# Two MLPs that apply their norm after the first product, with split inputs made during the projection ahead, in a two-layer transformer kernel

## The chip, the cores and the metric

The kernel runs on one core of one Trainium2 chip, as one program. The metric is its device time in microseconds (us). All inputs and outputs are float32.

## The reference

The model has a first block of two layers (a mixer of neighbourhood attention and mLSTM heads, then an RWKV-7 mixer, each followed by an MLP) and a second block with a mixture of experts. What the change touches is the MLP of both layers and the end of the mixer ahead of it:

```python
def rms_norm(x, eps=NORM_EPS):
    xf = x.astype(jnp.float32)
    return (xf * lax.rsqrt(jnp.mean(xf * xf, axis=-1, keepdims=True) + eps)).astype(x.dtype)

def modulate(x, shift, scale):
    return rms_norm(x) * (1.0 + scale) + shift

def adaln(cond, w, b):
    return jnp.split(jax.nn.silu(cond) @ w + b, 6, axis=-1)

def squared_relu_mlp(h, w1, w2):
    return jnp.square(jax.nn.relu(h @ w1)) @ w2

# in each layer; the context only in the first
x = x + gt_a * o_l                # o_l ends with the mixer's output projection
x = x + gt_m * squared_relu_mlp(modulate(x, sh_m, sc_m), mlp_w1[layer], mlp_w2[layer])
ctx = ctx + cgt_a * o_c
ctx = ctx + cgt_m * squared_relu_mlp(modulate(ctx, csh_m, csc_m), mlp_w1[layer], mlp_w2[layer])
```

The width is 1024, the MLP's hidden width 4096. There are 512 tokens and 256 context tokens, with a shift, scale and gate of their own for the context.

## The kernel before

Activations lie transposed: 8 tiles `x[k]` of 128 features by 768 columns (512 tokens, then 256 of the context). `PARTS` is ((0, 512), (512, 768)), and layer 1's MLP works on the first part alone.

**Dense products.** Every float32 factor is split in a high and a low part, and a product is three matmuls: wh·ah, wh·al, wl·ah (`dense`, L493 in the trace). A weight tile (128 outputs, 1024 inputs) comes by DMA on SP's queue, ScalarE (ACT) makes `wh` (L471) and GpSimd (POOL) `wl` (L472). There are two buffers for split weights, so ACT can split the next tile only when TensorE (PE) has finished with the one before the last. Output tiles go to PSUM, into two accumulators of 768 columns (`wide`); in layer 0 a matmul for 512 and one for 256 columns follow each other on the same weight.

**Output projections.** `po` (layer 0, in `ab_mixer`) and `ro` (layer 1, in `rw_mixer`): eight output tiles each. Behind each, VectorE (DVE) adds gate times the tile to x (`residual`, L584), and `squares_add` squares x on ACT and sums over the eight tiles in `acc`. Behind the last, PE adds the sums over the partitions (`ssc`, L549), a chain of small steps on DVE and ACT takes the root (`rsv`, `rsy`), and PE turns it into rows (`rstd`, L559).

**MLP.** `modulate` makes eight pairs `ah`, `al` from x, the norm, scale and shift. Then four groups: eight up tiles of 128 hidden features, ReLU out of PSUM (ACT), squaring (DVE L616), split in `hh` (ACT) and `hl` (DVE L472), and eight down tiles `dn` with a residual each. The first two up tiles advance together (`dense_pair`).

**Conditioning passes.** Beside the MLP, `ada_side` makes the six adaLN vectors of the next layer. A step loads a tile of 128 x 1024 (`wside`, two buffers) and does one pass on DVE (L460, 128 x 1024 with a sum), or two for the vectors that the context needs too, 64 passes in 48 steps for each MLP. One step stands behind each up and down tile in the code.

**What sets the order.** The code is written stage by stage, and a scheduler (`tc`, tile pools) reorders instructions on each engine by when it reckons that their inputs and buffers are ready; each engine then takes its own list in order. A pool's memory comes free when the pool is closed. In `ab_mixer` the order of the heads is written by hand (`AB_ORDER`), and the splits `ch`, `cl` of the mixer's output `cat` come from the heads' own pool.

Of the kernel before, what the change touches and what calls it, by code (L numbers as in the profile page):

```python
# [10 lines left out]
F32 = mybir.dt.float32  # L11
# [4 lines left out]
ALU = mybir.AluOpType  # L16
# [275 lines left out]
PARTS = ((0, T), (T, TT))  # L292
NTD = 2
# [12 lines left out]
class Kern:  # L306
# [86 lines left out]
    def wide(self, name="a"):  # L393
        return self.acc.tile([128, TT], F32, tag="acc", name=self.uid(name))
# [47 lines left out]
    def ada_side(self, layer, pool):  # L442
# [8 lines left out]
        def step(j, f):  # L451
            n = 2 if j < 2 else 1
            if f == 0:
                self.ada[layer, j] = self.const.tile([128, 8, 2], F32, name=f"ada{layer}_{j}")
            out = self.ada[layer, j]
            w = pool.tile([128, D], F32, tag="wside", name=self.uid("wside"), bufs=2)
            nc.sync.dma_start(w, self.i[f"ada{layer}"][8 * j + f])
            for q in range(n):
                o = pool.tile([128, D], F32, tag="side", name=self.uid("side"), bufs=1)
                nc.vector.scalar_tensor_tensor(o, w, 1.0, cb[:, q, :], op0=ALU.mult, op1=ALU.mult, accum_out=out[:, f, q:q + 1])  # L460
            if f == 7:
# [4 lines left out]
        return [lambda j=j, f=f: step(j, f) for j in (1, 0, 2, 4, 3, 5) for f in range(8)]  # L466


    def split(self, src, hi, lo, eng=None):
        nc = self.nc  # L470
        nc.scalar.activation(hi, src, AF.Copy)  # L471
        (eng or nc.vector).tensor_tensor(lo, src, hi.bitcast(F32), op=ALU.subtract)  # L472
# [11 lines left out]
    def dense(self, ps, w, act, parts, k0=0, first=True, last=True):  # L484
# [96 lines left out]

    def residual(self, x, ps, gt, f, parts):
        for q, (a, b) in enumerate(parts):
            self.nc.vector.scalar_tensor_tensor(x[:, a:b], ps[:, a:b], gt[:, f, q:q + 1], x[:, a:b],  # L584
                                                op0=ALU.mult, op1=ALU.add)


    def mlp(self, layer, parts):
# [3 lines left out]
        with tc.tile_pool(name=f"mlp{layer}", bufs=2, reuse_waits="tile") as pool:  # L592
# [6 lines left out]
            act = self.modulate(self.x, sh, sc, parts, pool)  # L599
            w1, w2 = self.i[f"mlp1_{layer}"], self.i[f"mlp2_{layer}"]  # L600

            first = self.dense_pair("up", [w1[0], w1[1]], act, parts)

            def up(g):
                hid = []
                for f in range(8 * g, 8 * g + 8):
                    if first:
                        ps = first.pop(0)
                    else:
                        ps = self.wide("up")  # L610
                        self.dense(ps, self.load_w(w1[f], 1024), act, parts)
# [14 lines left out]
            for g in range(4):  # L626
# [3 lines left out]
                for f in range(KD):  # L630
# [9 lines left out]
            self.tb = 6  # L640


    def ab_mixer(self):
# [24 lines left out]
        with ExitStack() as st:  # L668
            cp = st.enter_context(tc.tile_pool(name="ab_c", bufs=1, reuse_waits="tile"))
            pool = self.abp = st.enter_context(tc.tile_pool(name="ab", bufs=2, reuse_waits="tile"))  # L670
# [263 lines left out]
            for f in range(8):  # L934
                self.tap("cat", cat[f], f)
            act2 = []
            for f in range(8):
                h = pool.tile([128, TT], F32R, tag="ah", name=self.uid("ch"), bufs=KD)
                l = pool.tile([128, TT], F32R, tag="al", name=self.uid("cl"), bufs=KD)
# [4 lines left out]
            acc = tmp("acc")  # L944
# [1512 lines left out]
```

## Time and profile before

| | |
|---|---|
| times of three runs, us | 3525.28, 3518.22, 3511.94 |
| median, us | 3518.22 |
| the profiled execution's own time, us | 3523.28 |
| its span, us | 3521.4 |
| mean granted clock of TensorE | 0.961 of full speed |
| PE busy | 3171.4 us (90%) |
| DVE busy | 1820.7 us (52%) |
| ACT busy | 1320.0 us (37%) |
| POOL busy | 913.9 us (26%) |
| DMA in 40 equal slices of the span | 34th and 35th 274 GB/s, 36th to 39th 420 or 421, last 312, most others 60 to 190 |

The span is the time between the first and the last instruction of the profiled execution; 1.9 us lie around it. An engine's busy time is a mean over stages with different limits: here PE, which is busy 90% of the span, is the engine that others wait for in most of them. Times in rows count from the start of the span.

### The profile page before, as it was taken

The numbers are of one execution on the slowest core, as the hardware profiler recorded it, in microseconds if no ns is written. First come the engines' busy times: TensorE is split into PE (matmuls) and PEld (weight loads), VectorE is DVE, ScalarE is ACT, GpSimd is POOL, SyncE is SP. The second block draws the span as 40 slices with busy tenths as digits, with TensorE's granted clock in tenths as the row PEclk, the third lists the DMA queues.
The fourth block names the chain that finished last, engine by engine and source line by source line (L and its number), as shares of the span: only waits on it lengthen the run. The fifth ranks groups of instructions, "written<-read, shape, count | busy, mean of one in ns | idle before, by whom it ended". The sixth has DMA issues, their size and how long they took to land. (4 is left out here: it accounts for less than half of the span.)

```text
span 3521.4 us, 56690 instructions
## 1 busy us (share of the span) xinstructions
PE 3171.4 (90%) x23582; PEld 2413.3 (69%) x23582; DVE 1820.7 (52%) x3073; ACT 1320.0 (37%) x2503; POOL 913.9 (26%) x467
## 2 busy tenths in 40 slices
PE   7989998899999789589999998799999899799887
PEld 4666887788888677377887876677778677333333
DVE  5476664862322975477777763864342654222213
ACT  3232453211222543377777774322233453100001
POOL 1111113222324423422223212344443324100000
PEclk9999999999999899699999998999999999899999
DMA  5222222552222233200000103473332228799997
GB/s 220 96 72 84 84 73 96 186 185 66 64 63 98 85 106 109 69 18 28 28 28 28 31 8 114 161 251 126 94 115 67 75 78 274 274 420 421 420 421 312
DMA packets 126321, 488.44 MB, mean 139 GB/s; under 512 B 13360, under 2 KB 23024, under 8 KB 101744
## 3 DMA queue, kind: packets, MB, share of 16 engines
q1 hardware_dynamic: 119936, 477.40, 37.9%
q8 instruction: 186, 3.05, 0.4%
q0 software_dynamic: 1184, 4.20, 0.3%
q10 hardware_dynamic: 4944, 3.21, 0.3%
q14 instruction: 71, 0.58, 0.1%
HBM read 455.92 MB, written 28.84 MB: 138 GB/s over the span
## 5 line engine op out<-in xcount | busy, mean ns | idle before, releaser
L472 POOL TENSOR_TENSOR wl<-w,wh 128x1024 fp32r<-128x1024 f32 (+1 forms) x259 | 626.4, 2420 | 1602.2 <-ACT wh L471 1458.0
L471 ACT ACTIVATE wh<-w 128x1024 fp32r<-128x1024 f32 (+1 forms) x259 | 266.8, 1032 | 909.5 <-PE dn L493 333.6
L493 PE MATMUL dn<-hh,wh 128*128 128x512 f32 (+1 forms) x768 | 235.5, 361 | 18.3 <-ACT hh L471 16.5
L493 PE MATMUL up<-ah,wl 128*128 128x512 f32 (+1 forms) x768 | 235.9, 361 | 6.3 <-POOL wl L472 6.2
L493 PE MATMUL up<-ah,wh 128*128 128x512 f32 (+1 forms) x768 | 235.2, 361 | 5.9 <-ACT ah L576 2.8
L493 PE MATMUL dn<-hl,wh 128*128 128x512 f32 (+1 forms) x768 | 235.1, 360 | 2.3 <-DVE hl L472 2.3
L493 PE MATMUL dn<-hh,wl 128*128 128x512 f32 (+1 forms) x768 | 234.5, 359 | 2.3 <-POOL wl L472 2.2
L493 PE MATMUL up<-al,wh 128*128 128x512 f32 (+1 forms) x768 | 234.8, 360 | 0.9 <-DVE al L577 0.9
L460 DVE SCALAR_TENSOR_TENSOR side<-wside,condb 128x1024 f32<-128x1024 f32 x128 | 194.7, 1521 | 69.7 <-DMA wside<-ada 68.5
L616 DVE TENSOR_TENSOR u<-u 128x768 f32<-128x768 f32 (+1 forms) x64 | 126.9, 1986 | 128.8 <-ACT u L615 128.8
L584 DVE SCALAR_TENSOR_TENSOR x<-dn,ada,x 128x512 f32<-128x512 f32 x96 | 60.5, 657 | 255.6 <-PE dn L493 255.6
L493 PEld LDWEIGHTS dn<-hh,wh 128*128 128x128 f32 x768 | 128.5, 191 | 42.4 <-ACT hh L471 18.1
L493 PEld LDWEIGHTS up<-ah,wl 128*128 128x128 f32 x768 | 128.8, 191 | 31.6 <-POOL wl L472 10.0
L493 PEld LDWEIGHTS up<-ah,wh 128*128 128x128 f32 x768 | 129.2, 192 | 29.8 <-ACT ah L576 3.9
L493 PEld LDWEIGHTS dn<-hl,wh 128*128 128x128 f32 x768 | 128.6, 191 | 26.3 <-DVE hl L472 4.2
L493 PEld LDWEIGHTS dn<-hh,wl 128*128 128x128 f32 x768 | 128.5, 191 | 25.1 <-POOL wl L472 3.1
L493 PEld LDWEIGHTS up<-al,wh 128*128 128x128 f32 x768 | 128.8, 191 | 24.2 <-DVE al L577 2.0
L471 ACT ACTIVATE hh<-u 128x768 fp32r<-128x768 f32 (+1 forms) x64 | 47.3, 740 | 220.9 <-DVE u L616 220.9
L493 PE MATMUL p<-ah,wh 128*128 128x512 f32 (+1 forms) x320 | 116.9, 394 | 2.2 <-ACT ah L576 1.2
L493 PE MATMUL rp<-xl,wh 128*128 128x512 f32 x368 | 109.2, 361 | 10.5 <-DVE xl L472 10.4
L493 PE MATMUL rp<-xh,wh 128*128 128x512 f32 x368 | 109.6, 364 | 9.1 <-ACT xh L471 7.9
L493 PE MATMUL p<-ah,wl 128*128 128x512 f32 x320 | 112.7, 381 | 2.1 <-POOL wl L472 2.1
(623 smaller groups left out, 7427.9 us busy)
## 6 DMA issues: line engine op xcount, KB each, us to landing
w<-mlp SPq DMA_DIRECT2D x128, 512.0 KB, 3.7
wside<-ada SPq DMA_DIRECT2D x96, 512.0 KB, 4.1
ew<-e_gate SPq DMA_DIRECT2D x45, 1024.0 KB, 19.8
ew<-e_up SPq DMA_DIRECT2D x41, 1024.0 KB, 21.1
ew<-e_down SPq DMA_DIRECT2D x39, 1024.0 KB, 19.8
wada<-ada SPq DMA_DIRECT2D x48, 512.0 KB, 3.6
ewm<-e_up SPq DMA_DIRECT2D x18, 1024.0 KB, 20.0
ewm<-e_down SPq DMA_DIRECT2D x18, 1024.0 KB, 19.8
```

The costliest lines, as they stand in the source:

```text
L460: nc.vector.scalar_tensor_tensor(o, w, 1.0, cb[:, q, :], op0=ALU.mult, op1=ALU.mult, accum_out=out[:, f, q:q + 1])
L471: nc.scalar.activation(hi, src, AF.Copy)
L472: (eng or nc.vector).tensor_tensor(lo, src, hi.bitcast(F32), op=ALU.subtract)
L493: nc.tensor.matmul(ps[:, a:b], ww[:, 128 * k:128 * k + 128], aa[:, a:b], start=(first and k == 0 and q == 0), stop=(last and k == nk - 1 a ...
L584: self.nc.vector.scalar_tensor_tensor(x[:, a:b], ps[:, a:b], gt[:, f, q:q + 1], x[:, a:b], op0=ALU.mult, op1=ALU.add)
L616: nc.vector.tensor_tensor(u[:, lo:hi], u[:, lo:hi], u[:, lo:hi], op=ALU.mult)
```

## The change

Three things change.

**The norm's place.** The pairs `ah`, `al` are no longer made by `modulate` but by `scaled`, one pair behind each residual of the output projection, from x times scale, without the norm and the shift. The shift is two more columns of the same pairs, so each up product carries 2 columns more; its product with the weights is read from PSUM behind the last column. The norm's matmuls stand among the first up products (`between`): the sums behind the sixth of eight steps (of 128 inputs) of the first up tile, the turning into rows behind the fourth of the second. DVE multiplies each up tile by the norm's rows `rn`, and ACT's ReLU adds the shift's product as its bias. In layer 1 the up products no longer have 512 columns in one matmul but 256 and 258 in two (`SHIFTED`), 768 more matmuls in all; in layer 0 they have 512 and 258. The first two up tiles of an MLP are put down one behind the other.

**Conditioning passes.** A step is now one pass, so 64 steps. One stands behind each up tile, two behind each down tile of the first two groups and one behind the others, each held behind the split or residual ahead of it (`issue_after`).

**The heads' pool.** In `ab_mixer` the heads' pool is closed after the last head, and the splits `ch`, `cl` come from a new pool `abo` behind it.

```diff
+SHIFTED = {1: ((0, T // 2), (T // 2, T + 2, T)), 2: ((0, T), (T, TT + 2))}
@@ ada_side @@
-        return [lambda j=j, f=f: step(j, f) for j in (1, 0, 2, 4, 3, 5) for f in range(8)]
+        parts = {j: 2 if j < 2 else 1 for j in range(6)}
+        return [partial(step, j, f, q, parts[j]) for j in (1, 0, 2, 4, 3, 5) for f in range(8) for q in range(parts[j])]
@@ dense @@
-                for a, b in parts:
-                    nc.tensor.matmul(ps[:, a:b], ww[:, 128 * k:128 * k + 128], aa[:, a:b],
+                for a, b, *at in parts:
+                    at = at[0] if at else a
+                    nc.tensor.matmul(ps[:, at:at + b - a], ww[:, 128 * k:128 * k + 128], aa[:, a:b],
@@ new @@
+    def scaled(self, layer, k, parts):
+        nc = self.nc
+        sh, sc = self.ada[layer, 3], self.ada[layer, 4]
+        n, x = parts[-1][1], self.x[k]
+        h, l = (self.actp.tile([128, n + 2], F32R, tag=tag, name=self.uid(tag)) for tag in ("ah", "al"))
+        c = sh[:, k, :] if len(parts) == 2 else sh[:, k, 0:1].to_broadcast([128, 2])
+        nc.scalar.activation(h[:, n:], c, AF.Copy)
+        nc.vector.tensor_tensor(l[:, n:], c, h[:, n:].bitcast(F32), op=ALU.subtract)
+        for q, (a, b) in enumerate(parts):
+            nc.scalar.activation(h[:, a:b], x[:, a:b], AF.Copy, scale=sc[:, k, q:q + 1])
+            nc.vector.scalar_tensor_tensor(l[:, a:b], x[:, a:b], sc[:, k, q:q + 1], h[:, a:b].bitcast(F32),
+                                           op0=ALU.mult, op1=ALU.subtract)
+        self.act.append((h, l))
@@ mlp @@
-            act = self.modulate(self.x, sh, sc, parts, pool)
-            first = self.dense_pair("up", [w1[0], w1[1]], act, parts)
+            def norm_cols():
+                self.y = self.rstd_tokens(self.ss, parts)
+            def norm_rows():
+                for (a, b), r in zip(parts, self.rstd_banks(self.y, parts)):
+                    nc.scalar.activation(rn[:, a:b], r, AF.Copy)
+            between = {(0, 2): norm_cols, (1, 1): norm_rows}
+            def shifted(f):
+                ps = self.wide("up", TT + 2)
+                w = self.load_w(w1[f], 1024)
+                for k in range(0, KD, 2) if f < 2 else (0,):
+                    n = 2 if f < 2 else KD
+                    self.dense(ps, [t[:, 128 * k:128 * (k + n)] for t in w], self.act, SHIFTED[np_], k0=k,
+                               first=(k == 0), last=(k + n == KD))
+                    if (f, k // 2) in between:
+                        between[f, k // 2]()
+                return ps
+            def relu(ps, u):
+                b = self.small.tile([128, 2], F32, tag="shift", name=self.uid("shift"), bufs=4)
+                nc.vector.tensor_copy(b, ps[:, TT:TT + 2])
+                if np_ == 2:
+                    nc.vector.tensor_tensor(u, ps[:, :TT], rn, op=ALU.mult)
+                else:
+                    for p, a in ((0, 0), (T, T // 2)):
+                        nc.vector.tensor_tensor(u[:, a:a + T // 2], ps[:, p:p + T // 2], rn[:, a:a + T // 2], op=ALU.mult)
+                for q, (p, e) in enumerate(parts):
+                    nc.scalar.activation(u[:, p:e], u[:, p:e], AF.Relu, bias=b[:, q:q + 1])
+            first = [shifted(f) for f in range(2)]
+            def beside(ins, n=1):
+                with tc.issue_after(ins.ins):
+                    for _ in range(min(n, len(side))):
+                        side.pop(0)()
@@ up @@
-                    nc.scalar.activation(u[:, lo:hi], ps[:, lo:hi], AF.Relu)
+                    relu(ps, u)
                     nc.vector.tensor_tensor(u[:, lo:hi], u[:, lo:hi], u[:, lo:hi], op=ALU.mult)
-                    self.split(u[:, lo:hi], h[:, lo:hi], l[:, lo:hi])
+                    beside(self.split(u[:, lo:hi], h[:, lo:hi], l[:, lo:hi]))
-                    if side:
-                        side.pop(0)()
@@ down @@
-                    self.residual(self.x[f], ps, gt, f, parts)
+                    ins = self.residual(self.x[f], ps, gt, f, parts)
-                    if side:
-                        side.pop(0)()
+                    beside(ins, 2 if g < 2 else 1)
@@ ab_mixer @@
-            pool = self.abp = st.enter_context(tc.tile_pool(name="ab", bufs=2, reuse_waits="tile"))
+            heads = ExitStack()
+            pool = self.abp = heads.enter_context(tc.tile_pool(name="ab", bufs=2, reuse_waits="tile"))
...
+            heads.close()
+            pool = st.enter_context(tc.tile_pool(name="abo", bufs=KD, reuse_waits="tile"))
...
+            self.open_scaled()
+            acc = self.ss = self.actp.tile([128, TT], F32, name="ssq", bufs=1)
...
                 self.residual(self.x[f], ps, self.ada[0, 2], f, PARTS)
+                self.scaled(0, f, PARTS)
                 self.squares_add(acc, self.x[f], f, PARTS, tmp, nc.gpsimd)
-            self.y = self.rstd_tokens(acc, PARTS)
```

`rw_mixer` gets the same lines around `ro` (`open_scaled`, `scaled(1, f, LAT)`, no `rstd_tokens`).

The order of instructions moves at these places. First, DVE at the end of the last mLSTM head: `cat` is the mixer's output and `ch`, `cl` its split, `am` and `cst` belong to the recurrence of the heads. Before, rows stand in this order:

```order
L472 TENSOR_TENSOR cl_4560<-cat_364,ch_4559 128x768
L472 TENSOR_TENSOR cl_4564<-cat_365,ch_4563 128x768
L472 TENSOR_TENSOR cl_4568<-cat_366,ch_4567 128x768
L1041 TENSOR_TENSOR am_4343<-u_4347,cab 128x256
L1041 TENSOR_TENSOR am_4345<-u_4354,cab 128x256
L1041 TENSOR_TENSOR am_4343<-u_4361,cab 128x512
L1041 TENSOR_TENSOR am_4345<-u_4372,cab 128x512
L1065 COPY cst_4388<-cst_4383 128x130
```

Seven of the eight `cl` stand ahead of the last head's `am`. In the changed kernel DVE's list at the end of that head reads:

```order
L1159 TENSOR_SCALAR hsum_4489<-hsum_4489,rsy_4518 128x128 x6
L1167 SCALAR_TENSOR_TENSOR cat_367<-o_4330,params,ho_4533 128x512
L1167 SCALAR_TENSOR_TENSOR cat_367<-o_4330,params,ho_4539 128x256
L474 TENSOR_TENSOR cl_4549<-cat_360,ch_4548 128x768
L474 TENSOR_TENSOR cl_4553<-cat_361,ch_4552 128x768
L474 TENSOR_TENSOR cl_4557<-cat_362,ch_4556 128x768
```

All eight `cl` now stand behind the last `cat` (the first three are shown). Second, PE at the same head; `u`, `num` and `cst` are products of the recurrence, `ho` is the last product of a head, `po` the output projection. Before:

```order
L493 MATMUL po_4592<-ch_4547,wh_4595 128x256
L493 MATMUL po_4592<-cl_4548,wh_4595 128x512
L1040 MATMUL u_4361<-consts,mlc_u 128x128 x4
L1040 MATMUL u_4372<-consts,mlc_u 128x128 x4
L1055 MATMUL cst_4383<-mvt_4233,kt_4232 128x130
L493 MATMUL po_4592<-cl_4548,wh_4595 128x256
L493 MATMUL po_4592<-ch_4547,wl_4596 128x512
```

Now the projection's first product stands behind the head's last:

```order
L1125 MATMUL num_4483<-mvt_4233,am_4345 128x130
L1129 MATMUL num_4483<-cst_4472,qkraw_3903 128x130
L1166 MATMUL ho_4533<-consts,hsum_4489 128x128 x4
L1166 MATMUL ho_4539<-consts,hsum_4489 128x128 x2
L496 MATMUL po_4600<-ch_4548,wh_4603 128x512
L496 MATMUL po_4600<-ch_4548,wh_4603 128x256
L496 MATMUL po_4667<-ch_4548,wh_4670 128x512
```

Products of `po` stood among those of the recurrence, and no longer do. Third, DVE in the first up tiles of layer 0, between the squaring of one up tile `u` and that of the next; `side` is a conditioning pass. Before:

```order
L616 TENSOR_TENSOR u_5368<-u_5368 128x768
L460 SCALAR_TENSOR_TENSOR side_5513,ada_1_5293<-wside_5511,condb 128x1024
L472 TENSOR_TENSOR hl_5370<-u_5368,hh_5369 128x768
L460 SCALAR_TENSOR_TENSOR side_5515,ada_1_5293<-wside_5511,condb 128x1024
L460 SCALAR_TENSOR_TENSOR side_5581,ada_1_5293<-wside_5579,condb 128x1024
L460 SCALAR_TENSOR_TENSOR side_5583,ada_1_5293<-wside_5579,condb 128x1024
L460 SCALAR_TENSOR_TENSOR side_5649,ada_1_5293<-wside_5647,condb 128x1024
L616 TENSOR_TENSOR u_5436<-u_5436 128x768
```

And now, where `shift` is the copy of the two columns and `rn` the norm's rows:

```order
L652 COPY shift_5376<-up_5318 128x2
L654 TENSOR_TENSOR u_5373<-up_5318,rn 128x768
L677 TENSOR_TENSOR u_5373<-u_5373 128x768
L474 TENSOR_TENSOR hl_5375<-u_5373,hh_5374 128x768
L461 SCALAR_TENSOR_TENSOR side_5386,ada_1_5300<-wside_5384,condb 128x1024
L652 COPY shift_5446<-up_5388 128x2
```

Five passes stood between two squarings, and now one does, with a copy and a product with the norm added.

## Rows read from the trace of the kernel before

**Rows 1.** Timeline of ACT: start us, duration us, what; in brackets idle before, releaser

```profile
577.09 1.06 ACT L471 ACTIVATE wh<-w 128x1024 fp32r<-128x1024 f32 x1 [6.00 <-PE po L493]
...
1137.35 1.06 ACT L471 ACTIVATE wh<-w 128x1024 fp32r<-128x1024 f32 x1 [5.99 <-PE dn L493]
...
1145.67 1.06 ACT L471 ACTIVATE wh<-w 128x1024 fp32r<-128x1024 f32 x1 [5.99 <-PE dn L493]
...
2210.40 1.06 ACT L471 ACTIVATE wh<-w 128x1024 fp32r<-128x1024 f32 x1 [3.94 <-PE ro L493]
...
2603.54 1.06 ACT L471 ACTIVATE wh<-w 128x1024 fp32r<-128x1024 f32 x1 [3.78 <-PE dn L493]
...
2609.14 1.06 ACT L471 ACTIVATE wh<-w 128x1024 fp32r<-128x1024 f32 x1 [3.78 <-PE dn L493]
```

**Rows 2.** Stretches: us; PE, PEld, DVE, ACT, POOL busy; PE's clock; DMA share; GB/s

```profile
497.00:522.00 25.00, 24.72 (x173) 22.31 (x172) 17.59 (x62) 16.74 (x46) 2.39 (x1) 1.00 0.37 132
577.40:587.60 10.20, 3.40 (x19) 2.91 (x19) 5.65 (x12) 2.58 (x5) 2.35 (x1) 0.75 0.46 157
2210.40:2220.50 10.10, 3.14 (x13) 2.50 (x12) 5.50 (x11) 2.58 (x5) 2.35 (x1) 0.68 0.63 238
```

**Rows 3.** Waits of PE early in both MLPs: us, number, longest

```profile
PE dn L493 <- ACT hh L471: 8.5, 1, 8.5
...
PE dn L493 <- ACT hh L471: 4.4, 1, 4.4
...
PE dn L493 <- DVE hl L472: 1.1, 3, 0.6
```

**Rows 4.** Timeline of PE and DVE at the last head and the projection behind it

```profile
525.88 0.59 PE L493 MATMUL po<-ch,wh 128*128 128x512 f32 x2 [0.16 <-DVE x L584]
527.86 0.61 PE L493 MATMUL po<-ch,wl 128*128 128x512 f32 x2 [1.05 <-POOL wl L472]
...
491.00 7.20 DVE L472 TENSOR_TENSOR cl<-cat,ch 128x768 fp32r<-128x768 f32 x7
520.51 1.14 DVE L1099 SCALAR_TENSOR_TENSOR cat<-o,params,ho 128x512 f32<-128x512 f32 x2
```

**Rows 5.** Timeline of PE at the start of layer 1's output projection

```profile
2161.74 0.63 PE L493 MATMUL ro<-oh,wl 128*128 128x512 f32 x1
...
2166.01 0.48 PE L493 MATMUL ro<-oh,wh 128*128 128x512 f32 x1
```

**Rows 6.** Timeline of ACT: a one-column activation

```profile
527.88 0.19 ACT L536 ACTIVATE warm<-acc 128x1 f32<-128x1 f32 x1
```

**Rows 7.** Timeline of PE: the norm's matmuls ahead of both MLPs

```profile
581.44 1.86 PE L549 MATMUL ssc<-ones,acc 128*128 128x2 f32 x12 [4.09 <-DVE acc L541]
584.83 1.54 PE L559 MATMUL rstd<-consts,rsy 128*128 128x128 f32 x6 [1.53 <-DVE rsy L529]
...
2214.48 1.87 PE L549 MATMUL ssc<-ones,acc 128*128 128x2 f32 x8 [3.93 <-DVE acc L541]
```

**Rows 8.** Timeline of DVE in layer 0's first up tiles

```profile
653.63 0.95 DVE L616 TENSOR_TENSOR u<-u 128x768 f32<-128x768 f32 x1
...
656.51 3.46 DVE L460 SCALAR_TENSOR_TENSOR side<-wside,condb 128x1024 f32<-128x1024 f32 x1
...
660.01 1.23 DVE L460 SCALAR_TENSOR_TENSOR side<-wside,condb 128x1024 f32<-128x1024 f32 x1
```

**Rows 9.** One tile's weight loads: count, min/median/max ns, stretch in us

```profile
L493 PEld LDWEIGHTS po<-ch,wh x128: 186/188/245, 498.9 to 576.2; 128*128 128x128 f32 x128
```

**Rows 10.** Timeline of DVE: residuals in layer 1's first down group, first and last of eight

```profile
2289.44 0.75 DVE L584 SCALAR_TENSOR_TENSOR x<-dn,ada,x 128x512 f32<-128x512 f32 x1
...
2333.89 0.74 DVE L584 SCALAR_TENSOR_TENSOR x<-dn,ada,x 128x512 f32<-128x512 f32 x1
```

**Rows 11.** Timeline of PE: the recurrence in the heads, two products a row

```profile
509.94 0.39 PE L1057 MATMUL num<-mvt,am 128*128 128x130 f32 x2
510.16 0.39 PE L1061 MATMUL num<-cst,qkraw 128*128 128x130 f32 x2
```

More of the change, by code (lines that the diff above doesn't have):

```diff
@@ L449, in ada_side, with step @@
         bias = self.p("ada_b_20" if layer == 2 else f"ada_b{layer}")
-        def step(j, f):
-            n = 2 if j < 2 else 1
-            if f == 0:
+        def step(j, f, q, n, st={}):
+            if f == q == 0:
                 self.ada[layer, j] = self.const.tile([128, 8, 2], F32, name=f"ada{layer}_{j}")
             out = self.ada[layer, j]
[L456 to L461, printed above, removed]
+            if q == 0:
+                st["w"] = pool.tile([128, D], F32, tag="wside", name=self.uid("wside"), bufs=2)
+                nc.sync.dma_start(st["w"], self.i[f"ada{layer}"][8 * j + f])
+            o = pool.tile([128, D], F32, tag="side", name=self.uid("side"), bufs=1)
+            nc.vector.scalar_tensor_tensor(o, st["w"], 1.0, cb[:, q, :], op0=ALU.mult, op1=ALU.mult, accum_out=out[:, f, q:q + 1])
+            if f == 7 and q == n - 1:
                 nc.vector.scalar_tensor_tensor(out[:, :, :n], out[:, :, :n], 1.0 if j in (1, 4) else 0.0,
@@ L580, in modulate, with open_scaled @@
         return out
+    def open_scaled(self):
+        self.ast = ExitStack()
+        self.actp = self.ast.enter_context(self.tc.tile_pool(name=self.uid("act"), bufs=KD, side="right", reuse_waits="tile"))
+        self.act = []
+    def scaled(self, layer, k, parts):
[11 more added lines that the diff above has]
+        self.act.append((h, l))
     def residual(self, x, ps, gt, f, parts):
         for q, (a, b) in enumerate(parts):
-            self.nc.vector.scalar_tensor_tensor(x[:, a:b], ps[:, a:b], gt[:, f, q:q + 1], x[:, a:b],
-                                                op0=ALU.mult, op1=ALU.add)
+            ins = self.nc.vector.scalar_tensor_tensor(x[:, a:b], ps[:, a:b], gt[:, f, q:q + 1], x[:, a:b],
+                                                      op0=ALU.mult, op1=ALU.add)
+        return ins
     def mlp(self, layer, parts):
@@ L597, in tmp @@
                 return pool.tile([128, TT], F32, tag="tmp", name=self.uid(name), bufs=self.tb)
-            act = self.modulate(self.x, sh, sc, parts, pool)
             w1, w2 = self.i[f"mlp1_{layer}"], self.i[f"mlp2_{layer}"]
-            first = self.dense_pair("up", [w1[0], w1[1]], act, parts)
+            np_ = len(parts)
+            rn = pool.tile([128, TT], F32, name="rn", bufs=1)
+            def norm_cols():
[29 more added lines that the diff above has]
+                        side.pop(0)()
             def up(g):
@@ L606, in up @@
                 for f in range(8 * g, 8 * g + 8):
[L607 to L611, printed above, removed]
+                    ps = first.pop(0) if first else shifted(f)
                     u = pool.tile([128, TT], F32, tag="tmp", name=self.uid("u"), bufs=self.tb)
@@ L935, in ab_mixer, with tmp @@
                 self.tap("cat", cat[f], f)
+            heads.close()
+            pool = st.enter_context(tc.tile_pool(name="abo", bufs=KD, reuse_waits="tile"))
+            def tmp(name):
+                return pool.tile([128, TT], F32, tag="tmp", name=self.uid(name), bufs=6)
+            tmp("sq")
             act2 = []
             for f in range(8):
-                h = pool.tile([128, TT], F32R, tag="ah", name=self.uid("ch"), bufs=KD)
-                l = pool.tile([128, TT], F32R, tag="al", name=self.uid("cl"), bufs=KD)
+                h = pool.tile([128, TT], F32R, tag="ah", name=self.uid("ch"))
+                l = pool.tile([128, TT], F32R, tag="al", name=self.uid("cl"))
                 self.split(cat[f], h, l)
@@ L1306, in rw_mixer @@
                 first = self.dense_pair("ro", [wo[0], wo[1]], act, LAT, ws)
-                acc = pool.tile([128, T], F32, name="acc", bufs=1)
+                self.open_scaled()
+                acc = self.ss = self.actp.tile([128, TT], F32, name="ssq2", bufs=1)
                 for f in range(KD):
```

10 lines of the change are left out of this document (5 added, 5 removed).

## The prediction

> **What bounds the kernel now.** I read the stretches first, then the rows in order of time. TensorE (PE) carries both MLPs. ScalarE (ACT) splits a weight tile as soon as PE has finished the tile that used the buffer, so these rows mark the ends of PE's tiles [rows 1]: a tile takes 8.32 us in layer 0 (1137.35 to 1145.67) and 5.60 us in layer 1 (2603.54 to 2609.14). Layer 0's output projection ends at 577.09 and its MLP at 1145.67, so 568.6 us for 64 tiles that need 64 x 8.32 = 532.5: **36.1 us lost**. Layer 1: 2210.40 to 2609.14, 398.7 us for 64 x 5.60 = 358.4: **40.3 us lost**. The losses sit in two places. Before each MLP PE stands or works on the norm for some 10 us, and the granted clock is down (0.75 and 0.68 on average) [rows 2]. In the first tiles after that VectorE (DVE) has more conditioning passes than it can fit between the tiles, and the first down tile waits 8.5 and 4.4 us for its last hidden tile [rows 3]. In the last sixth of the span the experts' loads keep the DMA engines full (the table of times), but they start out of the second block, behind the second MLP, so a shift there carries through to the end.
>
> The place that the change also touches is the end of the first mixer. While the last mLSTM head runs, PE is busy 24.72 of 25.00 us at full clock [rows 2], because seven of eight input tiles of the output projection were split early (DVE, 491.00) and PE puts products of it between those of the head. So the third output tile starts already at 525.88, although the last input exists only at 520.51 + 1.14 = 521.65 [rows 4].
>
> **The change, part by part.** Base is the profiled execution's own 3523.3 us (span 3521.4); the median of the runs shown is 3518.2, 5.1 lower.
>
> *Output projection of layer 0: +14.3.* The split tiles of the mixer's output move to a pool that opens after the heads' pool is closed. In the new order all eight splits stand behind the last head's `cat` on DVE, and PE's first product of `po` behind the last `ho`. So the work no longer fills the head. The first split is ready at 521.65 + 1.03 (7.20 / 7 [rows 4]) = 522.7. Two tiles take 16.6. PE, then idle ahead of them, restarts at the lower clock: after such a pause ten products took from 2161.74 to 2166.01, 0.427 us each where 0.233 is the later rate (5.60 / 24) [rows 1, 5], so about eleven of them lose 2.1. The third tile starts at 541.4 instead of 525.88: +15.5. The 1.2 us that it waited there for its weights (its second such row stands at 527.86) should go: +14.3. Bounds: +11.5 without a slow restart and with a head that runs 0.5 faster for lack of other work, +21 in the third rival. The seven splits and eight tiny ones on DVE are then hidden by PE's 16.6 us.
>
> *Shift columns: +1.2.* Eight copies of two columns stand on ACT ahead of the weight splits with which layer 1's output projection starts. The nearest row, one column, is 0.19 us [rows 6]; overlapped I take 0.15 each. Bounds 0.8 and 1.5. In layer 0 the same eight stand behind the splits, under running products: nothing.
>
> *MLP of layer 0: -31.1.* The products start from x times scale, already split while the projection's later tiles run; that costs 0.9 us on ACT and 1.0 on DVE in 8.32 and is hidden. The norm's matmuls remain, now inside PE's stream: 1.86 + 1.54 [rows 7]. Two more columns on 768 products: 768 x 2 / 2400 = 0.6 us. DVE's tile becomes a two-column copy (0.19, the nearest row is ACT's of one column), the product with the norm, squaring and low part (0.95 each, 768 columns, the row of the squaring), and one pass of 1.23: 4.3 us [rows 6, 8]. One of them may wait for GpSimd's weight split; such a pass took 3.46 instead of 1.2 [rows 8], so 6.5 at most, below 8.32. Before, up to five passes stood between two squarings. The passes' 48 loads are the same; SP issues each between weight loads, which can stand behind one that waits for its buffer, but the buffer's last pass is then a tile or two old and three weight buffers give two tiles of room: nothing. The 8.5 us wait and the later ones on accumulators go, and I leave 1.0 for what is not foreseen. New loss 3.4 + 0.6 + 1.0 = 5.0 instead of 36.1. Bounds 3 and 8.
>
> *MLP of layer 1: -26.4.* The norm's matmuls: 1.87 and four turns in place of six, 1.54 x 4 / 6 = 1.03, so 2.9 [rows 7]. The ones-product stands after six of eight steps, 4.2 us after the start. Before, it could start 4.08 after the projection's end (2214.48), and the last tile's low part, about 0.6, now stands ahead of the sum on DVE: a wait near 0.7 with its hops. The hand-over from up to down cost 1.1 us in three where no passes were left [rows 3]: four make 1.5. A lag of DVE in the down tiles with two passes: 3.0 (between 0 and 12, second rival). Then the split of each 512-column product in 256 and 258 columns, 768 of them. A product of 512 costs 5.60 / 24 = 0.2333 us, 0.0200 above its columns. Layer 0's pair of 512 and 256 costs 8.32 / 24 = 0.3467, 0.0267 above its 768 columns. That pair is the nearest row, two products on one weight tile: 514 / 2400 + 0.0267 = 0.2408, +0.0075 x 768 = +5.8. Bounds: each half at what the 256 adds in layer 0 (0.1133), -4.5; each with its own 0.0200, +16.0. New loss 2.9 + 0.7 + 1.5 + 3.0 + 5.8 = 13.9 instead of 40.3. Bounds 1.5 and 30.
>
> The Trainium skill (TensorE: Matmul & The Clock Gate, Back-to-back issue gap) gives a product its columns over 2.4 GHz plus 2.5 ns. By that the split would cost 3.4 ns (219.2 against 215.8), an estimate of +2.6 us and 3 us off the total; the rows show 20 ns, not 2.5, above the columns, so I keep them.
>
> Sum: 14.3 + 1.2 - 31.1 - 26.4 = **-42.0**, so 3481.3 on the profile's base and 3476.2 on the median's. I forecast **3479**, between.
>
> **The rivals.** *Slower: weight loads come to light.* Every product carries its own load, recorded at 186 to 188 ns [rows 9]. If two short products on one tile can't hide them, a pair costs 0.376 instead of 0.2333: 0.143 x 768 = +110 in place of 5.8, 3479 + 104 = 3583. It decides from a pair of 0.2333 + (42.0 + 5.8) / 768 = 0.296 us on. Against it: in layer 0 the load behind a 256-column product is hidden already, since that product adds only 0.113. The Trainium skill (same page, LDWEIGHTS) has a load take its columns over 1.2 GHz, 107 ns for 128; by that the halves just hide it, and no row here shows a load's length apart from its waiting.
>
> *Passes still bind in layer 1.* The eight residuals of its first down group stand 6.35 us apart ((2333.89 - 2289.44) / 7) [rows 10] while PE needs 5.60, because passes wait for two load buffers. PE wasn't held, for the lag stayed within the second accumulator. If it does hold PE in the 16 down tiles of the first two groups: 16 x 0.75 = 12, 9 more than counted: 3488. For it: the new order has exactly two passes behind each residual; against it: before it were more than two.
>
> *A slow last head.* Without the filling, PE's clock may fall inside the head. Its recurrence sends three pairs of products a step, 0.22 us a pair (509.94 to 510.16) [rows 11], ten steps, each twice as long at 1.2 GHz: 10 x 3 x 0.22 = +6.6, so 3486. Against it: these products alone keep PE busy in the steps. The rule that an idle array is throttled to half its clock is in the Trainium skill (TensorE: Matmul & The Clock Gate, Part 1); the trace agrees around both norms, and whether a half-filled head counts as idle no row of this kernel shows.
>
> *The first products don't move up.* PE takes its rows in order, and if sums, table load or condition vector come late on DVE or ACT, the gap returns behind six steps instead of ahead of them: 10.2 + 10.1 [rows 2] and two restarts of 2.1, +24.5: 3503.
>
> **Numbers.** Forecast 0.58, passes 0.14, slow head 0.14, first products 0.08, loads 0.06. Half a per cent (17.6 us) is about what a measurement of this kernel can tell from no change: faster means below 3500.6. The first three are faster, 0.86; the fourth the same, 0.08; the fifth slower, 0.06. With all lower bounds the sum is 3523.3 + 11.5 + 0.8 - 33.1 - 38.8 = 3463.7, on the median 3458.6; with all upper ones 3523.3 + 21 + 1.5 - 28.1 - 10.3 = 3507, on the median 3502. Range 3458 to 3505, the first four cases.
>
> **What the new profile would show.** Right: no `po` product before the last `ho`, low PE activity in the last 8 us of the head, a projection that ends near 591. Then the first `up` product right behind the last `po` at full clock, one pass between squarings, the first down tile unheld, an MLP of about 537 us, and one of about 372 in layer 1 with up tiles near 5.8. Wrong: up tiles of layer 1 above 6.5; down tiles above 5.6; PE waiting for `rn` or `ssq`; the head longer than 25 us.

## The result and the profile after

| | before | changed |
|---|---|---|
| median, us | 3517.19 (4 runs) | 3473.95 (4 runs) |
| lowest and highest, us | 3511.94, 3525.28 | 3466.93, 3476.39 |
| the profiled execution's own time, us | 3523.28 | 3474.30 |
| its span, us | 3521.4 | 3472.5 |
| mean granted clock | 0.961 | 0.968 |
| PE, DVE, ACT busy, us | 3171.4, 1820.7, 1320.0 | 3156.7, 1913.4, 1343.7 |

The changed kernel takes 0.9872 of the time before, 95% interval 0.9856 to 0.9888: 43.2 us less by the medians. By the spans it is 48.9, since the profiled execution of before lies 6.1 above its median.

These rows of ACT in the changed kernel answer to [rows 1]; they are the weight splits that mark the ends of PE's tiles.

```profile
644.47 1.06 ACT L473 ACTIVATE wh<-w 128x1024 fp32r<-128x1024 f32 x1 [3.23 <-PE up L496]
652.93 1.06 ACT L473 ACTIVATE wh<-w 128x1024 fp32r<-128x1024 f32 x1 [3.23 <-PE up L496]
...
1130.61 1.06 ACT L473 ACTIVATE wh<-w 128x1024 fp32r<-128x1024 f32 x1 [6.00 <-PE dn L496]
...
2234.51 1.06 ACT L473 ACTIVATE wh<-w 128x1024 fp32r<-128x1024 f32 x1 [0.96 <-PE up L496]
2240.24 1.06 ACT L473 ACTIVATE wh<-w 128x1024 fp32r<-128x1024 f32 x1 [0.97 <-PE up L496]
...
2559.76 1.06 ACT L473 ACTIVATE wh<-w 128x1024 fp32r<-128x1024 f32 x1 [3.80 <-PE dn L496]
```

An up tile of layer 0 now takes 8.46 us (644.47 to 652.93) and one of layer 1 5.73; before, all tiles took 8.32 and 5.60. Layer 0's MLP ends at 1130.61 and layer 1's at 2559.76. Where they start stands in PE's timeline:

```profile
591.42 0.51 PE L496 MATMUL po<-ch,wl 128*128 128x512 f32 x2
591.77 0.51 PE L496 MATMUL up<-ah,wh 128*128 128x512 f32 x2
...
598.11 1.39 PE L552 MATMUL ssc<-ones,ssq 128*128 128x2 f32 x12
...
605.83 0.81 PE L562 MATMUL rstd<-consts,rsy 128*128 128x128 f32 x6
...
2191.57 0.40 PE L496 MATMUL ro<-oh,wl 128*128 128x512 f32 x1
2191.80 0.40 PE L496 MATMUL up<-ah,wh 128*128 128x256 f32 x2
...
2196.55 1.05 PE L552 MATMUL ssc<-ones,ssq 128*128 128x2 f32 x8 [0.29 <-DVE ssq L544]
...
2201.84 0.60 PE L562 MATMUL rstd<-consts,rsy 128*128 128x128 f32 x4
```

The first row of up products follows the last row of `po` by 0.35 us, as rows of two products do inside either stream, and the first up product of layer 1 follows the last of `ro` by 0.23: the stops are gone. So layer 0's MLP runs from 591.7 to 1130.6, 539.0 us where it took 568.6, and layer 1's from the last product of `ro` to the last of `dn` takes 367.9 us where it took 398.7. The norm's matmuls stand inside the stream at full clock, where `ssc` takes 1.39 instead of 1.86 and `rstd` 0.81 instead of 1.54. In the stretches that answer to [rows 2] (the same columns; the last head, then the first 10 us of either MLP) PE fell back in the first one and is full in the others:

```profile
497.00:523.40 26.40, 15.50 (x107) 14.06 (x106) 15.46 (x58) 19.02 (x48) 2.35 (x1) 0.86 0.07 20
591.70:601.90 10.20, 10.20 (x64) 9.12 (x63) 5.82 (x12) 3.55 (x6) 2.40 (x1) 1.00 0.50 165
2191.80:2201.90 10.10, 9.81 (x82) 9.60 (x81) 4.87 (x10) 4.77 (x6) 4.18 (x2) 1.00 0.61 237
```

What PE waits for in layer 1's MLP (us, number, longest) is 1.7 us in all, against 8.5 and 4.4 in single waits of [rows 3]; for layer 0's MLP the view is empty:

```profile
PE dn L496 <- DVE hl L474: 0.9, 4, 0.2
PE up L496 <- DVE u L657: 0.5, 1, 0.5
PE ssc L552 <- DVE ssq L544: 0.3, 1, 0.3
```

DVE's up tile in layer 0, where five passes stood between two squarings, is now copy, product, squaring, low part and one pass, and then it is free for 1.4 us:

```profile
627.85 0.16 DVE L652 COPY shift<-up 128x2 f32<-128x2 f32 x1 [1.38 <-PE up L496]
627.92 0.95 DVE L654 TENSOR_TENSOR u<-up,rn 128x768 f32<-128x768 f32 x1
630.07 1.83 DVE L677 TENSOR_TENSOR u<-u 128x768 f32<-128x768 f32 x1 [1.19 <-ACT u L659]
632.81 0.96 DVE L474 TENSOR_TENSOR hl<-u,hh 128x768 fp32r<-128x768 f32 x1 [0.91 <-ACT hh L473]
633.69 1.22 DVE L461 SCALAR_TENSOR_TENSOR side<-wside,condb 128x1024 f32<-128x1024 f32 x1
...
636.31 0.16 DVE L652 COPY shift<-up 128x2 f32<-128x2 f32 x1 [1.39 <-PE up L496]
```

The residuals that stood 6.35 us apart [rows 10] stand (2285.89 - 2246.78) / 7 = 5.59 apart, the pace of PE's tiles:

```profile
2246.78 0.75 DVE L608 SCALAR_TENSOR_TENSOR x<-dn,ada,x 128x512 f32<-128x512 f32 x1
...
2285.89 0.75 DVE L608 SCALAR_TENSOR_TENSOR x<-dn,ada,x 128x512 f32<-128x512 f32 x1 [0.39 <-PE dn L496]
```

### The profile page after: what moved, and what is told of

It reads as the page before. It is cut to its first block, busy times and chain, and to the rows that moved or that the text cites. A ratio compares the mean times of both kernels' runs of the same rounds, so it can differ in the third digit from the quotient of the medians.

```text
span 3472.5 us, 58491 instructions
## 1 busy us (share of the span) xinstructions
PE 3156.7 (91%) x24350; PEld 2444.2 (70%) x24350; DVE 1913.4 (55%) x3225; ACT 1343.7 (39%) x2554; POOL 927.9 (27%) x467
## 5 line engine op out<-in xcount | busy, mean ns | idle before, releaser
L474 POOL TENSOR_TENSOR wl<-w,wh 128x1024 fp32r<-128x1024 f32 (+1 forms) x259 | 633.9, 2449 | 1538.8 <-ACT wh L473 1415.9
L461 DVE SCALAR_TENSOR_TENSOR side<-wside,condb 128x1024 f32<-128x1024 f32 x128 | 231.1, 1806 | 17.8 <-DMA wside<-ada 16.6
L496 PE MATMUL up<-ah,wh 128*128 128x258 f32 (+2 forms) x1024 | 234.8, 310 | 0.5 <-DVE u L657 0.5
L496 PE MATMUL up<-al,wh 128*128 128x258 f32 (+2 forms) x1024 | 234.7, 310 | 0.0
L496 PE MATMUL up<-ah,wl 128*128 128x258 f32 (+2 forms) x1024 | 234.6, 310 | 0.0
L496 PEld LDWEIGHTS up<-ah,wh 128*128 128x128 f32 x1024 | 158.5, 189 | 12.0 <-issue 0.7
L496 PEld LDWEIGHTS up<-ah,wl 128*128 128x128 f32 x1024 | 158.2, 189 | 11.4
L496 PEld LDWEIGHTS up<-al,wh 128*128 128x128 f32 x1024 | 158.2, 189 | 11.0
L677 DVE TENSOR_TENSOR u<-u 128x768 f32<-128x768 f32 (+1 forms) x64 | 110.3, 1724 | 61.1 <-ACT u L659 61.1
L2465 ACT ACTIVATE xT<-ed,tcol 128x512 fp32r<-128x512 f32 (+1 forms) x17 | 11.2, 661 | 272.1 <-issue 183.5
```

What stands on the lines that cost most here:

```text
L461: nc.vector.scalar_tensor_tensor(o, st["w"], 1.0, cb[:, q, :], op0=ALU.mult, op1=ALU.mult, accum_out=out[:, f, q:q + 1])
L474: return (eng or nc.vector).tensor_tensor(lo, src, hi.bitcast(F32), op=ALU.subtract)
L496: nc.tensor.matmul(ps[:, at:at + b - a], ww[:, 128 * k:128 * k + 128], aa[:, a:b], start=(first and k == 0 and q == 0), stop=(last and k = ...
L2465: nc.scalar.activation(yh[:, s], pd[hf][:, cut], AF.Copy, scale=tcol[:, 0, p:p + 1])
```

## The experiments

The table has the medians (us; one run of e6) and three stages of the profiled execution: layer 0's MLP (from the last product of `po` to the weight split that marks its last tile's end), the output projection `ro` (first product to last), and layer 1's MLP (last product of `ro` to last product of `dn`). With every tile at its full pace and no stop, the MLPs would take 532.5 and 358.4.

| kernel | median | MLP 0 | `ro` | MLP 1 |
|---|---|---|---|---|
| before | 3518.2 | 568.6 | 53.7 | 398.7 |
| changed | 3473.95 | 539.0 | 50.9 | 367.9 |
| e1, before with bounded passes | 3479.9 | 548.4 | 53.7 | 375.1 |
| e2, changed with old passes | 3524.1 | 562.2 | 51.0 | 393.9 |
| e3, changed with the head's filling | 3459.1 | 539.0 | 50.1 | 368.3 |
| e4, layer 1 with one 512-column matmul, no shift | 3471.3 | 539.0 | 51.3 | 364.5 |
| e5, layer 1 with 512 and 2 columns | 3551.5 | 539.0 | 51.0 | 446.6 |
| e6, before with eight small copies | 3511.4 | 564.9 | 50.7 | 397.9 |
| e7, e1 without the hold | 3520.1 | 566.6 | 53.8 | 400.0 |
| e8, e3 with old passes | 3511.0 | 559.7 | 51.3 | 391.3 |
| e9, before with whole steps, held | 3489.4 | 547.2 | 53.5 | 383.5 |
| e10, e3 with the norm's place left to the scheduler | 3461.05 | 542.0 | 51.4 | 368.4 |

The kernel before had medians of 3518.16 beside e1 to e4, 3518.74 beside e5 to e8, and 3518.93 beside e9 and e10.

**e1, the bounded passes alone.** The kernel before gets the changed `ada_side` and `beside`, nothing else (the places where a step is put are shown):

```diff
-                    self.split(u[:, lo:hi], h[:, lo:hi], l[:, lo:hi])
+                    beside(self.split(u[:, lo:hi], h[:, lo:hi], l[:, lo:hi]))
-                    if side:
-                        side.pop(0)()
...
-                    self.residual(self.x[f], ps, gt, f, parts)
+                    ins = self.residual(self.x[f], ps, gt, f, parts)
-                    if side:
-                        side.pop(0)()
+                    beside(ins, 2 if g < 2 else 1)
```

> The kernel before with the bounded conditioning passes alone. Theory (the two losses of each MLP add up): what remains of layer 0's 36.1 us is the stop ahead of the first up tile, 10.5, and a slow restart of 2 with a small wait for the first split tiles, about 14; of layer 1's 40.3 about 16. So about 46 us less than before, near 3471, as much as the whole change, because the head's filling is kept. Rival (the passes bind only because the norm's elementwise work stands in the same stretch): bounding them alone gives half of that or less, 3495 or more.

Measured 3479.9, ratio 0.9879 (0.9861 to 0.9896): 38.3 us less than before, without the norm's new place. Layer 0's MLP lost 15.9 instead of 36.1, layer 1's 16.7 instead of 40.3, close to the 14 and 16 expected; by median the gain is 8 short of what the theory gave. The waits of 8.5 and 4.4 us for `hh` are gone, and the longest that PE has left in either MLP is the one for the sums of the norm (4.1 and 3.9). The rival falls.

**e2, the late norm with the old passes.** `ada_side` is that of the kernel before, and its steps stand where they stood (shown):

```diff
-                    beside(self.split(u[:, lo:hi], h[:, lo:hi], l[:, lo:hi]))
+                    self.split(u[:, lo:hi], h[:, lo:hi], l[:, lo:hi])
+                    if side:
+                        side.pop(0)()
...
-                    beside(ins, 2 if g < 2 else 1)
+                    if side:
+                        side.pop(0)()
```

> The changed kernel with the conditioning passes put as before: 48 steps of one or two passes, one behind each tile, none held behind a split. Theory: the waits of the first down tiles and accumulators come back, some 20 us in each MLP, about 3505 to 3515, close to the kernel before. Rival: without the norm's elementwise work VectorE has room for the passes, and the waits stay small: 3475 to 3485.

3524.1, ratio 1.0014 (1.0005 to 1.0024): not a gain at all, and 50 us behind the changed kernel. PE's waits in layer 0's MLP (us, number, longest) are back, for up tiles that DVE's passes hold:

```profile
PE up L496 <- DVE u L654: 4.5, 2, 2.5
PE dn L496 <- ACT hh L473: 3.8, 1, 3.8
PE dn L496 <- DVE x L608: 2.2, 1, 2.2
```

**e3, the head's filling kept.** The split tiles go to a pool that is opened below the heads' and so survives it; the memory that the scaled inputs need comes from closing the heads' pool above. Not shown is that `modulate` in `ab_mixer` also takes its pairs from the new pool, so that the splits of `cat` use the same buffers again.

```diff
+            keep = st.enter_context(tc.tile_pool(name="abk", bufs=KD, reuse_waits="tile"))
             pool = self.abp = heads.enter_context(tc.tile_pool(name="ab", bufs=2, reuse_waits="tile"))
...
-            heads.close()
-            pool = st.enter_context(tc.tile_pool(name="abo", bufs=KD, reuse_waits="tile"))
             act2 = []
             for f in range(8):
-                h = pool.tile([128, TT], F32R, tag="ah", name=self.uid("ch"))
-                l = pool.tile([128, TT], F32R, tag="al", name=self.uid("cl"))
+                h = keep.tile([128, TT], F32R, tag="ah", name=self.uid("ch"))
+                l = keep.tile([128, TT], F32R, tag="al", name=self.uid("cl"))
                 self.split(cat[f], h, l)
                 act2.append((h, l))
+            heads.close()
+            pool = st.enter_context(tc.tile_pool(name="abo", bufs=2, reuse_waits="tile"))
```

> The changed kernel with the split tiles of the mixer's output in a pool that stands below the heads' pool, so that seven of eight splits and their products can again stand among the last head's. Theory: the output projection ends 14 to 15 us earlier and nothing else changes: about 3459. Rival: the end of the head is bound by its own chain of small steps on VectorE and ScalarE, and the products in it lengthen that chain, so that less than half comes back: 3467 or more.

3459.1, ratio 0.9829 (0.9812 to 0.9847) to before and 14.8 us under the changed kernel: the fastest of all. The last `po` product stands at 576.0, where before had 577.1 and the changed kernel 591.7 (e8 and e10, with the same pool, have 580.0 and 579.0). Its stretches at the last head and behind the projection:

```profile
497.00:522.00 25.00, 24.72 (x170) 22.27 (x169) 17.11 (x62) 16.71 (x52) 2.39 (x1) 1.00 0.37 132
576.10:586.10 10.00, 10.00 (x63) 8.96 (x62) 5.68 (x11) 3.35 (x6) 2.40 (x1) 1.00 0.54 206
```

The head is as full as in [rows 2] (24.72 of 25.00), and there is no stop behind the projection either.

**e4 and e5, the shape of layer 1's up products.** e4 leaves out layer 1's shift, its two columns and the second matmul; e5 keeps both, with other borders. The first added line is e4's, the second e5's; in both, VectorE reads the product from where it then lies:

```diff
-SHIFTED = {1: ((0, T // 2), (T // 2, T + 2, T)), 2: ((0, T), (T, TT + 2))}
+SHIFTED = {1: ((0, T),), 2: ((0, T), (T, TT + 2))}
...
+SHIFTED = {1: ((0, T), (T, T + 2, TT)), 2: ((0, T), (T, TT + 2))}
```

> The changed kernel with layer 1's up products of 512 columns in one matmul; it leaves out layer 1's shift (the two extra columns and their matmuls). Theory: a product falls from the pair's time to 0.2333 us; the prediction's 0.2408 gives 5.8 us less, 3468; the pair seen in the changed kernel's trace, about 0.238, gives 3.5 less, 3470. Rival (the pair also hides or exposes weight loads and waits elsewhere): a change of over 8 us either way.

3471.3, 2.6 less than the changed kernel; in the stage itself 3.4, as the changed kernel's trace had it. The prediction's 5.8 was too high.

> The changed kernel with layer 1's up products as 512 and 2 columns instead of 256 and 258: the same columns and the same number of matmuls and weight loads, but almost no time behind the second load. If weight loads are hidden only behind a long enough product (the mechanism of the rival that would have made the change slower), a pair goes from 0.238 us towards 0.30 or more, 768 x 0.06 = 46 us or more: 3520 or slower. If a second product on the same weights costs only its own overhead, the pair stays near 0.238 and the time near 3474.

3551.5, ratio 1.0092 (1.0073 to 1.0111), slower than before. ACT's weight splits show an up tile of 8.26 us where the changed kernel has 5.73:

```profile
2225.07 1.06 ACT L473 ACTIVATE wh<-w 128x1024 fp32r<-128x1024 f32 x1 [3.54 <-PE up L496]
...
2233.33 1.06 ACT L473 ACTIVATE wh<-w 128x1024 fp32r<-128x1024 f32 x1 [3.53 <-PE up L496]
```

(8.26 - 5.73) / 24 = 0.105 us a pair, 768 pairs: 81 us, and 77.5 were measured by the medians. Columns, matmuls and weight loads are the same in number; only what runs while the next load goes on is shorter. This is the mechanism of the rival that would have made the change slower, with 2 columns instead of 258 to hide behind. A pair of 8.26 / 24 = 0.344 stands 0.111 above the product of 512 (0.2333). The Trainium skill (TensorE: Matmul & The Clock Gate, LDWEIGHTS) gives a load of 128 columns 107 ns, and that is about what comes to light here, where the loads' own rows show 188 with their waiting.

**e6, the eight copies alone.** In the kernel before, ahead of layer 1's output projection:

```diff
+                cols = pool.tile([128, 2 * KD], F32R, name="cols", bufs=1)
+                for k in range(KD):
+                    nc.scalar.activation(cols[:, 2 * k:2 * k + 2], self.ada[1, 3][:, k, 0:1].to_broadcast([128, 2]), AF.Copy)
                 first = self.dense_pair("ro", [wo[0], wo[1]], act, LAT, ws)
```

> The kernel before with eight copies of two columns on ScalarE ahead of the weight splits with which layer 1's output projection starts, where the changed kernel has its shift copies; their result is not used. Prediction's step: they delay the projection by 1.2 us, from 53.7 (first product to last) or its start to later. Theory from the trace of the changed kernel: they hold back the weight splits, so GpSimd's part starts after VectorE's product that took 2.73 us beside it and 0.69 without; the projection's span falls from 53.7 to about 51 us.

The projection took 50.7 us instead of 53.7. First the kernel before, DVE, POOL and PE:

```profile
2155.61 2.73 DVE L1438 TENSOR_TENSOR end<-y,g 128x512 f32<-128x512 f32 x1
...
2155.02 5.52 POOL L472 TENSOR_TENSOR wl<-w,wh 128x1024 fp32r<-128x1024 f32 x2 [86.12 <-ACT wh L471]
...
2156.47 0.80 PE L493 MATMUL ro<-oh,wh 128*128 128x512 f32 x1 [5.13 <-ACT oh L471]
2161.15 0.80 PE L493 MATMUL ro<-ol,wh 128*128 128x512 f32 x1 [3.89 <-DVE ol L472]
```

DVE's product for `end` (2155.61) starts together with POOL's weight split (2155.02) and takes 2.73 us, so the first `ol` is late and PE waits 3.89 us for it. In e6 the copies stand ahead of the weight splits on ACT, so POOL's part starts 0.17 us behind `end` and no longer ahead of it; `end` takes 0.69, and PE waits 1.11:

```profile
2142.71 0.84 ACT L1308 ACTIVATE cols<-ada 128x2 fp32r<-128x2 f32 x8
...
2144.41 0.69 DVE L1441 TENSOR_TENSOR end<-y,g 128x512 f32<-128x512 f32 x1
...
2144.58 5.53 POOL L472 TENSOR_TENSOR wl<-w,wh 128x1024 fp32r<-128x1024 f32 x2 [85.05 <-ACT wh L471]
...
2146.02 0.79 PE L493 MATMUL ro<-oh,wh 128*128 128x512 f32 x1 [5.88 <-ACT oh L471]
2147.92 0.79 PE L493 MATMUL ro<-ol,wh 128*128 128x512 f32 x1 [1.11 <-DVE ol L472]
```

The 2.8 us that PE waits less are nearly all of the 3.0 that the projection is shorter. The changed kernel shows the same with its own copies: `end` ends before POOL begins.

```profile
2137.67 0.69 DVE L1507 TENSOR_TENSOR end<-y,g 128x512 f32<-128x512 f32 x1
...
2139.18 5.16 POOL L474 TENSOR_TENSOR wl<-w,wh 128x1024 fp32r<-128x1024 f32 x2 [86.49 <-ACT wh L473]
...
2142.14 0.80 PE L496 MATMUL ro<-ol,wh 128*128 128x512 f32 x1 [0.73 <-DVE ol L474]
```

The Trainium skill (SBUF — State Buffer, Who interferes with whom) says that a VectorE instruction with two SBUF inputs contends with a GpSimd instruction that reads SBUF, and that the one which issues first goes ahead; 2.73 against 0.69 agrees, and so do the passes of 3.46 against 1.23 in [rows 8].

**e7 and e9, size of a step or hold.** e7 is e1 with one pass a step but without the hold; e9 has the old whole steps (up to two passes, 48 in all, one behind each tile), held. The edit shown is e7's against e1:

```diff
-                with tc.issue_after(ins.ins):
-                    for _ in range(min(n, len(side))):
-                        side.pop(0)()
+                for _ in range(min(n, len(side))):
+                    side.pop(0)()
```

> The kernel before with conditioning passes split into single steps, one behind each up tile and two or one behind each down tile in the code, but not held behind the split or residual. Theory: the scheduler pulls passes forward to wherever their weights are there, as before, and the hold is what counts: 3505 to 3520. Rival: one pass a step is enough: 3480.

3520.1, ratio 1.0003 (0.9993 to 1.0013): nothing is left of e1's gain. DVE in layer 0's up tiles has five passes between two squarings, as before:

```profile
654.60 0.95 DVE L622 TENSOR_TENSOR u<-u 128x768 f32<-128x768 f32 x1
655.47 1.22 DVE L459 SCALAR_TENSOR_TENSOR side<-wside,condb 128x1024 f32<-128x1024 f32 x1
...
657.49 3.47 DVE L459 SCALAR_TENSOR_TENSOR side<-wside,condb 128x1024 f32<-128x1024 f32 x1
...
661.01 1.23 DVE L459 SCALAR_TENSOR_TENSOR side<-wside,condb 128x1024 f32<-128x1024 f32 x1
...
662.27 1.22 DVE L459 SCALAR_TENSOR_TENSOR side<-wside,condb 128x1024 f32<-128x1024 f32 x1
...
663.54 1.22 DVE L459 SCALAR_TENSOR_TENSOR side<-wside,condb 128x1024 f32<-128x1024 f32 x1
...
664.69 0.95 DVE L622 TENSOR_TENSOR u<-u 128x768 f32<-128x768 f32 x1
```

> The kernel before with its 48 whole steps (one or two passes each), one behind each up and down tile, but each held behind the split or residual ahead of it. Theory (the hold counts, not the step's size): up to two passes stand between two squarings, 2.5 us in a tile of 8.32 or 5.60, so nearly all of the bounded passes' gain stays: 3475 to 3490. Rival (two passes are too many, above all in layer 1's tiles): 3495 or more.

3489.4, ratio 0.9923 (0.9906 to 0.9939). In layer 0 the whole steps cost nothing (547.2 against e1's 548.4); in layer 1 they cost 8.4, with a wait of the first down tile that e1 does not have:

```profile
PE dn L493 <- ACT hh L471: 4.1, 1, 4.1
```

So the hold is most of it, 29.5 us against the kernel before, and the single pass a step, with two steps behind each early down tile, is worth some 9 us more, in layer 1's shorter tiles: either theory had a part of it.

**e8, the late norm with the head's filling and old passes** (the edits of e2 on e3).

> Late norm with the head's filling kept and the conditioning passes as before: the fourth corner beside the kernel before, bounded passes alone, and both. Theory (the late norm is worth some 10 us in each MLP less what passes take back, and the head's loss of 14 is separate): about 3510, 14 less than late norm with old passes and without the filling. Rival: passes now collide earlier, and nothing is gained over the kernel before: 3518.

3511.0, ratio 0.9969 (0.9959 to 0.9978): as expected, 13 less than e2. So the late norm with nothing lost at the head gains 7.7 us on the old passes. In the profiled execution the MLPs are 8.9 and 7.4 us shorter and `ro` 2.4, and a part of that is lost again elsewhere (`po` ends 2.9 later). What the old passes cost stays: layer 0's MLP still loses 27.2 and layer 1's 32.9.

**e10, the norm's matmuls left to the scheduler.**

```diff
-            between = {(0, 2): norm_cols, (1, 1): norm_rows}
+            between = {}
+            norm_cols()
+            norm_rows()
```

> The changed kernel with the head's filling kept, and the norm's matmuls written ahead of the first up products and left to the scheduler, which puts 22 and 11 of layer 0's first products ahead of the sums and the turning. Theory: the products need no norm, so the place matters only while the sums or the root are still on their way: a wait of a few us in each MLP, 3459 to 3466. Rival: TensorE takes its list in order and the stop of the kernel before comes back, 20 us: 3479.

3461.05, ratio 0.9835 (0.9819 to 0.9851), 1.9 above e3 (PE's rows have 22 products ahead of the sums and 9 more ahead of the turning in layer 0). Layer 0's MLP takes 3.0 us longer, with a wait of 1.3 for the sums. The place written by hand is worth at most a few us, and the stop does not come back: no product needs the norm.

## Why the prediction held, step by step

The forecast was 3479, 39 us less by the medians; 43.2 came. The sum of the terms was -42.0, and the three stages with the end of `po` give 14.6 - 2.7 - 29.6 - 30.8 = -48.5 of the spans' -48.9. So the forecast is right in its main mechanisms, wrong in one small term, and 6.5 short in its sum.

- **Output projection of layer 0: +14.3, measured 14.6** (577.1 to 591.7), and e3 gives it back. In other executions of the same code the end lay at 588.7 to 591.2 (e2, e4, e5), and that of the old code at 575.1 to 578.6 (e1, e6, e7, e9); the means are 13.0 apart. The second tile ends at 541.75 where 541.4 was worked out, and that this is so close is partly luck, as two errors in it cancel. One rival had a small part:

```profile
505.83 0.64 PE L1123 MATMUL cst<-mvt,kt 128*128 128x130 f32 x2
506.26 0.64 PE L1125 MATMUL num<-mvt,am 128*128 128x130 f32 x2
...
514.44 0.39 PE L1129 MATMUL num<-cst,qkraw 128*128 128x130 f32 x2
...
523.46 1.63 PE L496 MATMUL po<-ch,wh 128*128 128x512 f32 x4
...
523.42 1.14 DVE L1167 SCALAR_TENSOR_TENSOR cat<-o,params,ho 128x512 f32<-128x512 f32 x2 [0.29 <-PE ho L1166]
```

The first pairs of the recurrence go at 0.43 us each (505.83 to 506.26) where full clock gives 0.22 [rows 11], so the clock did fall inside the half-filled head, but it was back after a few of them. `cat` is there at 523.42 + 1.14 = 524.56 instead of the 521.65 that the sum took over from before. Of these 2.9 us, 1.9 lie ahead of the head: the attention's first product, also named `po`, already stands at 106.7 and not at 104.8. So the slow head cost about 1 us, not 6.6. Against that, PE did not wait for the last `cat` and its split, as the sum had it, but began at 523.46 (522.7 was worked out) with products of `ch`, so that two tiles from there took 18.3 where 18.7 was counted.
- **Shift columns at `ro`: +1.2, measured -2.7 in the projection.** This step failed. The copies do hold back the weight splits, as it said, but it counted only the queue behind them on ACT. What they held back was POOL's part, which had been slowing a DVE product that PE waited for; e6 shows it. The chain from POOL over DVE to PE stood in no term.
- **MLP of layer 0: -31.1, measured -29.6.** The mechanism is right; the two shift columns were sized at 0.6 and cost 32 x (8.46 - 8.32) = 4.5, and the norm takes about 2.2 instead of 3.4, since it now runs at full clock. These two are all that is left of the loss of 6.5; the 1.0 set aside was not needed.
- **MLP of layer 1: -26.4, measured -30.8.** Three sizes were off: the pair of 256 and 258 costs 3.4 (e4) and not 5.8; the norm with its wait 1.9 and not 3.6; the lag of DVE nothing (residuals 5.59 apart) where 3.0 was set. At the hand-over PE waits 0.9 where 1.5 was set, but the down tiles take 2.7 more than 32 x 5.60 in all. With a wait of 0.5 for `u` that makes 8.5 of the 9.5 us that are lost now. The bounds of 1.5 and 30 were narrower than the bounds of their own terms, which add up to 0.6 and 33.1. The estimate by the Trainium skill (TensorE: Matmul & The Clock Gate, Back-to-back issue gap) was 2.6 for the pair, nearer to the 3.4 than the 5.8 from the rows.
- **What carried the gain** was not separated in the prediction, whose terms put stop and passes into one number for each MLP. e1 and e8 separate them: bounded passes -38.3, late norm -7.7 with the filling kept, +5.9 as it was put (e2). By stages the two add up: the late norm takes 8.9 and 7.4 us from the MLPs with the old passes, 9.4 and 6.8 with the bounded ones.
- **What stays open.** By medians the two together give 59.0 (e3), 13 more than 38.3 + 7.7. In the profiled executions 8 of it lie between layer 0's MLP and `ro`, where TensorE has the same products in every kernel, and 4 ahead of layer 0's MLP. The time from the end of layer 0's MLP to the first product of `ro` goes with how long the granted clock stands at 1.2 GHz there: up to 107.6 us in the four traces that take 1005.6 to 1006.9 (e3, e6, e7, e10), 112.4 to 113.7 in those that take 1008.9 to 1010.0 (changed, e2, e5, e9), and 116.6 to 122.1 in those that take 1010.8 to 1012.5 (before, e1, e4, e8). The groups do not follow the change (e7 and e3 are in the quickest, the kernel before and e8 in the slowest), so most of the 13 us need not come from it. Why the clock stayed low longer in one execution than in another was not tried.
- **The rivals.** First products that don't move up: no, their rows stand 0.35 and 0.23 us behind the projection's last; of the signs of being wrong, the wait for `ssq` is there, with 0.3 us. Passes that bind in layer 1: no. Weight loads that come to light: not at 256 and 258 columns, but at 2 (e5); where between them it begins was not tried.

## What to carry to other kernels

A filler that a scheduler may pull forward can cost more than the stop that one sees in the trace: count how many of them stand between two instructions on which the next engine waits, and hold each behind its place; that alone gave 29.5 us here (e9), and 38 with one pass a step (e1). When work is moved to win one stop, look at what its memory displaces: the late norm's new pool took away 14 us of filling in the stage ahead, and a pool opened below the heads' gave it back. Before a product is cut in two, check that each piece is long enough to hide the next weight load: 768 pairs of 256 and 258 columns cost 3.4 us more than 768 products of 512, pairs of 512 and 2 cost 82.

## What the runs showed of the hardware that was not expected

Eight copies of two columns on ScalarE made a projection 3.0 us shorter (53.7 to 50.7), because they moved the start of a GpSimd subtraction behind that of a VectorE product with two SBUF inputs (2.73 against 0.69 us). Two more columns on the second matmul of a pair cost more than their columns: 8.46 instead of 8.32 for 24 pairs is 5.8 ns a pair, where 2 columns at 2.4 GHz are 0.8. What makes up the rest was not tried.
